# A bidirectional RWKV-7 chunk scan on one Trainium2 core: separate PSUM banks for u and the state increment, an even timetable for two steps, and system transposes on GpSimd

## The chip, the cores and the metric

The kernel runs on one core of a Trainium2 chip. The metric is the device time of one execution in microseconds (us), lower is better. Each kernel is run several times and the median counts; a separate profiled execution supplies the trace from which durations and waits are read.

## The reference

The reference is a two-layer encoder trunk in fp32, applied to a prompt of 256 tokens and a sample of 1024 tokens with the same weights (width 1024, 16 heads of 64). Layer 0 mixes tokens with bidirectional RWKV-7, layer 1 with neighbourhood attention, and each is followed by a squared-ReLU MLP. Only the recurrence of layer 0 matters here; it runs once forwards and once backwards and the two outputs are added:

```
def _wkv_scan(r, w, k, v, a, b, reverse):
    def step(S, inp):
        r_t, w_t, k_t, v_t, a_t, b_t = inp
        sa = jnp.einsum('bhvk,bhk->bhv', S, a_t)
        S = S * w_t[:, :, None, :] + sa[..., None] * b_t[:, :, None, :] + v_t[..., None] * k_t[:, :, None, :]
        return S, jnp.einsum('bhvk,bhk->bhv', S, r_t)
    ...
    _, y = lax.scan(step, s0, seq, reverse=reverse)
...
for d in range(2):
    ...
    y = y + _wkv_scan(rf, _heads(decay), k_d, vf, -kk, kk * iclr, reverse=(d == 1))
...
y = ((y - mu) * lax.rsqrt(var + GN_EPS)).reshape(B, T, C) * lnx_g + lnx_b
y = y + (bonus * vf).reshape(B, T, C)
```

## The kernel before

The program does the trunk stage by stage: projections of RWKV-7, the scan, output projection and MLP, then attention and its MLP. Large products are three fp32r products (`ps<-ah,whi`, `ps<-al,whi`, `ps<-ah,wlo`), lines 95 to 97. The change touches only the scan stage.

The scan turns the recurrence over tokens into one over chunks of 64 tokens. Two heads share 128 partitions. It has ten jobs of 16 steps each: jobs 0 and 1 are the prompt (four head pairs of four chunks each), jobs 2 to 9 the sample (one head pair, 16 chunks each). In a step both directions advance by a chunk, direction d=1 about half a step behind d=0. One step of one direction is this chain:

- `s0` (L989, TensorE): `w` in PSUM receives the masked key products `zk` times the values.
- `sd` (L993, GpSimd): the state `S` times the chunk's decay.
- `s1` (L1000, TensorE): `w` += `ar`·`S`. Then two ACT (ScalarE) copies of `w` into `up` (L1004, in the profile `u<-w`).
- `s2` (L1009, TensorE): `us` = `Q`·`up`, where `Q` is the inverse of the chunk's triangular system. ACT copies it to `hv` (L1011) and, in two pieces by `s2c`, to `u2` (L1018, `u<-us`).
- `s3` (L1023, TensorE): the state increment from `lt` and `hv`. Two DVE (VectorE) operations add it to `sd` and make the new `S` (L1031; L1029 where a sequence begins). The next `s1` needs it.
- `s4` (L1037, TensorE): `w` += `zb`·`u2`. The output rows go to `y`, by ACT (L1040) in the first eight steps of a job, by DVE (L1042) in the last eight.

`us` and the state increment of direction d lie in one PSUM bank, `pbank[d]`, as columns 0 to 127 and 192 to 319.

Between these steps stands work for steps and jobs to come. A group is four chunks of a direction, and every two steps one group of each of these kinds is done: products `aps` (L807) and the DVE mask that makes `zb` (L809); products `kps` (L932), an ACT copy to `zk` (L935) and its GpSimd mask (L937); four transposes `lps` (L945) and the ACT copy `lt` (L948); two merges of small products, `yps` (L893, ACT copies L898) and `qps` (L908, ACT copies L912 into `Q`). The triangular systems of the next job are inverted once per job in 31 rank-1 updates on DVE (`tmp` L847, `q` L849, sizes up to 128x256). Ahead of them four copies transpose the system from `mraw` to `mt` (L836), behind them four more transpose the result to `qt` (L861); `qt` goes to DRAM and twelve DMAs (`qld`) bring it back as `Q` and `qx`. After a job its output is normalised half by half (`scan_post`): DVE and GpSimd work, a reciprocal root that goes between DVE and ACT (L1144, L1156 to L1159), four transposes `zps` (L1131) and an ACT copy `zt` (L1133).

The order is written by hand. Each piece of work is put in a list with a time in steps (`at(t, f)`, job j begins at 16j), the list is sorted, and under `manual_schedule` the instructions of TensorE, DVE, ACT and GpSimd stand in each queue exactly in that order. The numbers are thus no times on the chip; they only set the order, and an instruction at the head of its queue that waits holds all behind it. The DMA queue of SyncE (SP) takes its transfers in that order, too. PSUM tiles `aps`, `kps`, `lps`, `yps`, `qps`, `zps` share two pools of three buffers under one tag.

Of the kernel before, what the change touches and what calls it, by code (L numbers as in the profile page):

```python
# [48 lines left out]
class Trunk:  # L49
# [653 lines left out]
    def scan_begin(self):  # L703
# [11 lines left out]
                                           (("bb", 4), ("ar", 10), ("zb", 10)))  # L715
# [19 lines left out]
    def scan(self):  # L735
# [12 lines left out]
        grow(self.r_bk, fx, "bdk", [P, 4, P], 3)  # L748
# [4 lines left out]
        self.pbank = [self.pw.tile([P, 320], F32, name=f"us{d}") for d in range(2)]  # L753
# [18 lines left out]
    def scan_job(self, j):  # L772
# [13 lines left out]
        for n, (d, g) in enumerate(order):  # L786
# [26 lines left out]
            at(t - (1.614 if j else 7.0), load, E)  # L813
            for c in range(5):
                at(t + (c * 0.133 + -0.013 if c < 4 else 0.577), lambda c=c, f=prod: f(c), E)
            at(t + (1.263 if j else 1.011), store, E)
# [38 lines left out]
        def qst(i):  # L855
            q, r = J["q"], slice(8 * i, 8 * i + 8)
            if i == 0:
                J["qt"] = self.er.tile([P, 32, 32], F32, name="qt", tag="mraw")
                J["qd"] = self.dsc.tile([2, P, 32, 32], F32, name="qd", tag="qd", bufs=2)
                nc.sync.dma_start(J["qd"][0], q)  # L860
            nc.scalar.copy(J["qt"].rearrange("p s t -> p t s")[:, r], q[:, r])  # L861
            if i == 3:
                nc.sync.dma_start(J["qd"][1], J["qt"])
# [20 lines left out]
        for n, (d, g) in enumerate(order):  # L884
            m, c0 = grp[g]

            def merge1(d=d, g=g):
                lo, hi = d, 1 - d
                yps = self.pt.tile([64, 4, 32], F32, name="yps", tag="aps")
                for c in range(4):  # L890
                    for e in range(2):
                        r0 = 64 * e + 32 * lo
                        nc.tensor.matmul(yps[32 * e:32 * e + 32, c, :], J["zb"][d, g][r0:r0 + 32, c, 32 * hi:32 * hi + 32],  # L893
                                         J["qx"][r0:r0 + 32, 4 * g + c, :], start=True, stop=True)
                yt = self.rp.tile([P, 4, 32], F32, name="yt", tag="yt", bufs=2)
                for e in range(2):
                    rh = 64 * e + 32 * hi
                    nc.scalar.copy(yt[rh:rh + 32], yps[32 * e:32 * e + 32])  # L898
                J["yt", d, g] = yt

            def merge2(d=d, g=g):
                lo, hi = d, 1 - d
                Q, yt = J["Q"], J["yt", d, g]
                qps = self.pt.tile([P, 4, 32], F32, name="qps", tag="aps")
                for c in range(4):
                    for e in range(2):
                        rl, rh = 64 * e + 32 * lo, 64 * e + 32 * hi
                        nc.tensor.matmul(qps[rl:rl + 32, c, :], yt[rh:rh + 32, c, :],  # L908
                                         Q[rh:rh + 32, 4 * g + c, d, 32 * hi:32 * hi + 32], start=True, stop=True)
                for e in range(2):  # L910
                    rl = 64 * e + 32 * lo
                    nc.scalar.copy(Q[rl:rl + 32, 4 * g:4 * g + 4, d, 32 * hi:32 * hi + 32], qps[rl:rl + 32])  # L912
            t = 2 * n - 3.992
            at(t + 0.5833, merge1)
            at(t + 2.59, merge2)


            def kload(d=d, g=g, m=m, c0=c0):
                bk = self.rp.tile([P, 4, P], F32, name="bk", tag="bk", bufs=3)
# [7 lines left out]
            def kprod(c, d=d, g=g, n=n):  # L927
# [4 lines left out]
                nc.tensor.matmul(ps[:, c, :], bd[:, c, :], J["ar"][d, g][:, c, :], start=True, stop=True)  # L932
                if c == 3:
                    zk = self.rp.tile([P, 4, P], F32, name="zk", tag="zk", bufs=3)
# [5 lines left out]
            def ktr(c, d=d, g=g, n=n):  # L940
# [4 lines left out]
                nc.tensor.transpose(ps[:, c, :], bk[:, c, :], self.ident)  # L945
                if c == 3:
                    lt = self.rp.tile([P, 4, P], F32, name="lt", tag="lt", bufs=3)
# [25 lines left out]
        for d in range(2):  # L973
            for i in range(16):
# [4 lines left out]
                self.scan_step(at, i + 0.481 * d, J, st[d], d, cc, m, c0 + cc % 4, new, end, i >= 8)  # L979
        self.scan_post(at, J, grp, j == len(self.jobs) - 1)  # L980

    def scan_step(self, at, t, J, st, d, cc, m, ch, new, end, second):
# [23 lines left out]
        def s2():  # L1006

            us = self.pbank[d][:, 0:P]
# [6 lines left out]
        def s2c():  # L1015
            for e in range(2):
                es = slice(64 * e, 64 * e + 64)
                nc.scalar.copy(R["u2"][es, es], self.pbank[d][o:o + 64, es])  # L1018

        def s3():  # L1020

            sn = self.pbank[d][:, 192:320]
# [20 lines left out]
        at(t - 0.22, s0)  # L1043
        if not new and not end:
            at(t - 0.25, sd)
        at(t, s1)
        at(t + 0.33, s2)
        at(t + 0.33 + 0.01, s2c)
        if not end:
            at(t + 0.66, s3)  # L1050
        at(t + 0.82, s4)

    def scan_post(self, at, J, grp, last):

        nc = self.nc
        for half in range(2):
# [71 lines left out]
            def tr(st=st, yb=yb, runs=runs):  # L1128
                ps = self.pt.tile([P, 4, P], F32, name="zps", tag="aps")
                for b in range(4):  # L1130
                    nc.tensor.transpose(ps[:, b, :], yb()[:, b // 2, b % 2, :], self.ident)  # L1131
                zt = self.yp.tile([P, 4, P], F32, name="zt", tag="zt", bufs=1)
                nc.scalar.copy(zt, ps)  # L1133
                for m, k, tb in runs:
                    nc.sync.dma_start(self.scr["z_d"][m, :, tb * P:(tb + 2) * P], zt[:, k:k + 2].rearrange("p b t -> p (b t)"))
            for dt, f in ((-4.0 if tail else -1.5, ld), (-0.186, p1), (0.474, p2), (-0.5 if tail else 1.327, p3a), (1.601, p2b), (-0.4 if tail else 1.982, p3b), (1.843, p2c), (2.252, p3),
                          (3.521, p4), (4.15, p4b), (4.563, p5), (5.809, tr)):
# [787 lines left out]
```

## Time and profile before

| | before |
|---|---|
| median of 3 runs | 4403.65 us (4403.26 to 4409.92) |
| profiled execution, its own time | 4414.36 us |
| its span (first to last instruction) | 4412.6 us |
| mean granted TensorE clock | 0.948 |
| scan stage, first to last `s2` product | 820.2 to 1649.7 us |
| busy, share of the span | PE 92%, DVE 61%, ACT 41%, POOL 38% |

PE is TensorE's products and PEld its weight loads, DVE VectorE, ACT ScalarE, POOL GpSimd, SP the queue that issues most DMAs. A row of a view names the line, the engine, the operation and the tiles (out<-in), how many there were, their busy time and mean duration, and the idle time of the engine just before them with what ended it. A row of the timeline gives start and duration in us, the number of instructions drawn together (x2) and, in brackets, idle time before. A row of the windows gives busy time per engine and the granted clock (PEclk) between two times.

### The profile page before, as it was taken

The page shows a single profiled execution, that of the slowest core. Times are in us where ns is not written, and L with a number is a line of the kernel's source. Part 1 is how long each engine was busy: PE and PEld are TensorE (multiplying, and loading weights), DVE is VectorE, ACT ScalarE, POOL GpSimd, SP SyncE. Part 2 cuts the span into 40 slices and gives each one's busy share as a digit, 9 for nine tenths or more (in the row PEclk, how much of TensorE's full clock was granted, in tenths as well). Part 3 has the DMA queues.
Part 4 walks back from the last instruction along what each step waited for, and adds up shares of the span by engine and source line. Part 5 has one row for each costly group of instructions (what it writes and reads, how often), then busy time and mean ns, then how long its engine had stood idle before and what let it go on. Part 6 is the DMA issues. An engine that isn't in the chain of part 4 may idle for free.

```text
span 4412.6 us, 69989 instructions
## 1 busy us (share of the span) xinstructions
PE 4051.6 (92%) x25060; PEld 3365.7 (76%) x25060; DVE 2684.6 (61%) x5242; ACT 1797.0 (41%) x4785; POOL 1678.7 (38%) x1682
## 2 busy tenths in 40 slices
PE   7888989778888888999999999989998999999999
PEld 4665669667777767788888887977776888888888
DVE  7888873567767745755555556157666565555555
ACT  6764442566777773211111113256555311111111
POOL 5446663234444443422222224044445332222222
PEclk8996779899999999999999999999998999999999
DMA  3234455566566434111111112523334211111111
GB/s 117 81 106 167 167 175 153 149 146 145 139 152 146 116 86 158 58 39 39 39 39 39 39 39 87 167 63 71 77 74 146 86 36 37 39 39 39 39 39 58
DMA packets 484156, 400.27 MB, mean 91 GB/s; under 512 B 289152, under 2 KB 392480, under 8 KB 483808
## 3 DMA queue, kind: packets, MB, share of 16 engines
q1 hardware_dynamic: 447584, 328.56, 27.2%
q10 hardware_dynamic: 34416, 61.35, 3.8%
q0 software_dynamic: 1808, 5.90, 0.4%
q8 instruction: 197, 3.23, 0.3%
q14 instruction: 151, 1.24, 0.1%
HBM read 285.66 MB, written 121.24 MB: 92 GB/s over the span
## 4 chain that ended last, share of the span: by engine, by line
PE 62%; DVE 8%; ACT 6%; DMA 3%; issue 2%; SPq 2%; POOL 2%; ACTq 0%; DVEq 0%; POOLq 0%
PE ps L95 16%; PE ps L96 16%; PE ps L97 16%; PE us L1023 2%; DVE tmp L847 1%; DVE q L849 1%; PE kps L932 1%; PE vps L499 1%; PE op L1840 1%; DVE S L1031 1%; PE us L1009 1%; PE vps L501 1%; PE vps L500 1%; PE pt L1782 1%; PE aps L807 1%
## 5 line engine op out<-in xcount | busy, mean ns | idle before, releaser
L1397 DVE TENSOR_TENSOR x<-ps,x 128x256 f32<-128x256 f32 x1488 | 814.3, 596 | 638.4 <-PE ps L97 638.3
L95 PE MATMUL ps<-ah,whi 128*128 128x512 f32 (+1 forms) x2304 | 848.4, 368 | 4.2 <-ACT whi L89 3.5
L96 PE MATMUL ps<-al,whi 128*128 128x512 f32 (+1 forms) x2304 | 830.3, 360 | 2.6 <-POOL al L1287 2.6
L97 PE MATMUL ps<-ah,wlo 128*128 128x512 f32 (+1 forms) x2304 | 828.3, 360 | 2.1 <-POOL wlo L90 2.0
L90 POOL TENSOR_TENSOR wlo<-raw,whi 128x1024 fp32r<-128x1024 f32 (+1 forms) x178 | 390.4, 2193 | 861.6 <-ACT whi L89 834.2
L95 PE MATMUL ps<-hh,whi 128*128 128x512 f32 (+1 forms) x1536 | 548.3, 357 | 12.0 <-DVE x L1397 11.9
L96 PE MATMUL ps<-hl,whi 128*128 128x512 f32 (+1 forms) x1536 | 547.3, 356 | 0.0
L97 PE MATMUL ps<-hh,wlo 128*128 128x512 f32 (+1 forms) x1536 | 546.4, 356 | 0.0
L95 PEld LDWEIGHTS ps<-ah,whi 128*128 128x128 f32 x2304 | 439.1, 191 | 84.6 <-issue 13.4
L97 PEld LDWEIGHTS ps<-ah,wlo 128*128 128x128 f32 x2304 | 438.3, 190 | 72.3 <-POOL wlo L90 3.0
L96 PEld LDWEIGHTS ps<-al,whi 128*128 128x128 f32 x2304 | 439.3, 191 | 67.2 <-POOL al L1287 2.9
L89 ACT CAST whi<-raw 128x1024 fp32r<-128x1024 f32 (+1 forms) x206 | 200.4, 973 | 708.7 <-PE ps L96 639.0
L1376 POOL TENSOR_TENSOR rl<-rl 128x512 f32<-128x512 f32 (+1 forms) x192 | 174.3, 908 | 504.6 <-PE ps L97 462.5
L95 PEld LDWEIGHTS ps<-hh,whi 128*128 128x128 f32 x1536 | 291.5, 190 | 57.5 <-DVE x L1397 15.1
L1375 ACT ACTIVATE rl<-ps 128x512 f32<-128x512 f32 (+1 forms) x192 | 100.7, 525 | 550.1 <-PE ps L97 550.1
L97 PEld LDWEIGHTS ps<-hh,wlo 128*128 128x128 f32 x1536 | 292.0, 190 | 41.7
L96 PEld LDWEIGHTS ps<-hl,whi 128*128 128x128 f32 x1536 | 291.6, 190 | 40.5
L1378 ACT CAST hh<-rl 128x512 fp32r<-128x512 f32 (+1 forms) x192 | 105.6, 550 | 321.1 <-POOL rl L1376 321.0
L993 POOL TENSOR_TENSOR sd<-S,dall 128x128 f32<-128x128 f32 x256 | 118.4, 462 | 303.1 <-DVE S L1031 244.7
L1031 DVE SCALAR_TENSOR_TENSOR S<-us,dall,sd 64x64 f32<-64x64 f32 x512 | 144.6, 282 | 142.8 <-PE us L1023 75.0
L1379 DVE TENSOR_TENSOR hl<-rl,hh 128x512 fp32r<-128x512 f32 (+1 forms) x192 | 119.3, 621 | 150.4 <-ACT hh L1378 149.9
L1775 POOL TENSOR_TENSOR s<-s,mx 128x384 f32<-128x384 f32 (+1 forms) x154 | 116.9, 769 | 212.1 <-DVE mx L1774 136.5
(310 smaller groups left out, 8750.3 us busy)
## 6 DMA issues: line engine op xcount, KB each, us to landing
raw<-in_w_down_dram SPq DMA_DIRECT2D x64, 512.0 KB, 3.5
raw<-in_w_up_dram SPq DMA_DIRECT2D x64, 512.0 KB, 3.5
ar<-ar_d SPq DMA_DIRECT2D x80, 256.0 KB, 3.4
bk<-bk_d SPq DMA_DIRECT2D x80, 256.0 KB, 3.2
ar_d<-ar ACTq DMA_DIRECT2D x32, 512.0 KB, 2.7
bk_d<-bk ACTq DMA_DIRECT2D x32, 512.0 KB, 3.5
bs<-tab SPq DMA_DIRECT2D x128, 96.0 KB, 3.7
v_d<-vt ACTq DMA_DIRECT2D x80, 128.0 KB, 4.2
```

What stands on the lines that cost most here:

```text
L89: nc.scalar.copy(hi[:, cs], raw)
L90: lo_eng.tensor_tensor(out=lo[:, cs], in0=raw, in1=hi[:, cs].bitcast(F32), op=ALU.subtract)
L95: mm(ps, sh, mh, start=first, stop=False)
L96: mm(ps, sh, ml, start=False, stop=False)
L97: mm(ps, sl, mh, start=False, stop=last)
L993: nc.gpsimd.tensor_tensor(out=R["sd"], in0=st["S"], in1=self.dall[:, m, d, ch:ch + 1].to_broadcast([P, P]), op=ALU.mult)
L1031: nc.vector.scalar_tensor_tensor(out=S2[es, es], in0=sn[es, es], scalar=D, in1=R["sd"][es, es], op0=ALU.mult, op1=ALU.add)
L1376: nc.gpsimd.tensor_tensor(out=r[:, :n], in0=r[:, :n], in1=r[:, :n], op=ALU.mult)
L1378: nc.scalar.copy(hh[:, :n], r[:, :n])
L1379: nc.vector.tensor_tensor(out=hl[:, :n], in0=r[:, :n], in1=hh[:, :n].bitcast(F32), op=ALU.subtract)
L1397: nc.vector.tensor_tensor(out=xv, in0=ps[:, :n], in1=xv, op=ALU.add)
L1775: nc.gpsimd.tensor_tensor(out=s[:, :nk], in0=s[:, :nk], in1=mx[:, 2:3].to_broadcast([P, nk]), op=ALU.mult)
```

## The change

It is made of four parts.

1. `pbank[0]` and `pbank[1]` become `ubank` (all `us`) and `nbank` (all state increments), each shared by both directions.
2. The times change. Of a step: `s0` -0.22 to -0.12, `sd` -0.25 to -0.04, `s2c` 0.34 to 0.51, `s4` 0.82 to 0.717, the lag of d=1 0.481 to 0.5. The four products of a group stand at 0.05, 0.1, 0.27 and 0.43 of a step, `aps` in even steps, `kps` in odd ones; the mask that makes `zb` at 0.45, formerly 0.577 (the rank-1 updates stand at 0.43 of a step before, 0.47 after). The four transposes `lps` stand close together at 0.55 to 0.62. The ACT copies of `zk`, `lt`, `yt`, into `Q`, and `zt` get times of their own, behind the products that they read. `zps` and its copy move to steps 19.72 and 23.72, and the loads of the post-processing from `t0 - 1.5` to `t0 - 0.2`.
3. Buffers: `bb` 4 to 3, `bk` 3 to 2, `bdk` 3 to 2, `zk` and `lt` 3 to 4.
4. The eight transposing copies per job (`mtr` and `qst`, 64x256 and 128x256 fp32, read in rows and written with a stride of 32 elements) go from ACT to GpSimd.

Behind the change the lines of a step are: `s0` L1002, `sd` L1006, `s1` L1013, `up` L1017, `s2` L1022, `hv` L1024, `u2` L1031, `s3` L1036, `S` L1044 (or L1042), `s4` L1050, `y` L1053 and L1055; `kps` L943, `zk` L946 and L948, `lps` L957, `lt` L960, `yt` L902, `Q` L919, `zps` L1144.

```diff
-                                           (("bb", 4), ("ar", 10), ("zb", 10)))
+                                           (("bb", 3), ("ar", 10), ("zb", 10)))
...
-        self.pbank = [self.pw.tile([P, 320], F32, name=f"us{d}") for d in range(2)]
+        self.ubank, self.nbank = (self.pw.tile([P, P], F32, name=nm) for nm in ("us", "sn"))
...
-            at(t - (1.614 if j else 7.0), load, E)
-            for c in range(5):
-                at(t + (c * 0.133 + -0.013 if c < 4 else 0.577), lambda c=c, f=prod: f(c), E)
-            at(t + (1.263 if j else 1.011), store, E)
+            at(t - (1.614 if j else 5.0), load, E)
+            for c, dt in enumerate((0.05, 0.1, 0.27, 0.43, 0.45)):
+                at(t + dt, lambda c=c, f=prod: f(c), E)
+            at(t + 1.0, store, E)
...
-            nc.scalar.copy(J["mt"][64:128].rearrange("p s t -> p t s")[:, r], J["raw"][64:128, r])
+            nc.gpsimd.tensor_copy(J["mt"][64:128].rearrange("p s t -> p t s")[:, r], J["raw"][64:128, r])
...
-        T2 = T1 + (1.8 if j else 2.359)
+        T2 = T1 + (1.84 if j else 2.359)
...
-            nc.scalar.copy(J["qt"].rearrange("p s t -> p t s")[:, r], q[:, r])
+            nc.gpsimd.tensor_copy(J["qt"].rearrange("p s t -> p t s")[:, r], q[:, r])
...
-            t = 2 * n - 3.992
-            at(t + 0.5833, merge1)
-            at(t + 2.59, merge2)
+            t = 2 * n - 4
+            at(t + 0.55, merge1)
+            at(t + 1.2, merge1c)
+            at(t + 2.555, merge2)
+            at(t + 2.7, merge2c)
...
-            at(t - 2.665, kload)
-            for c in range(4):
-                at(t + c * 0.1667 + 0.7067, lambda c=c, f=kprod: f(c))
-                at(t + c * 0.242 + 1.448, lambda c=c, f=ktr: f(c))
+            t = 2 * n - 5
+            at(t - 1.75, kload)
+            for c, (dt, dl) in enumerate(((0.05, 0.55), (0.1, 0.57), (0.27, 0.6), (0.43, 0.62), (0.7, 1.2))):
+                at(t + dt, lambda c=c, f=kprod: f(c))
+                at(t + dl, lambda c=c, f=ktr: f(c))
...
-                self.scan_step(at, i + 0.481 * d, J, st[d], d, cc, m, c0 + cc % 4, new, end, i >= 8)
+                self.scan_step(at, i + 0.5 * d, J, st[d], d, cc, m, c0 + cc % 4, new, end, i >= 8)
...
-            us = self.pbank[d][:, 0:P]
+            us = self.ubank
...
-                nc.scalar.copy(R["u2"][es, es], self.pbank[d][o:o + 64, es])
+                nc.scalar.copy(R["u2"][es, es], self.ubank[o:o + 64, es])
...
-            sn = self.pbank[d][:, 192:320]
+            sn = self.nbank
...
-        at(t - 0.22, s0)
+        at(t - 0.12, s0)
         if not new and not end:
-            at(t - 0.25, sd)
+            at(t - 0.04, sd)
         at(t, s1)
-        at(t + 0.33, s2)
-        at(t + 0.33 + 0.01, s2c)
+        at(t + 0.333, s2)
+        at(t + 0.51, s2c)
         if not end:
-            at(t + 0.66, s3)
-        at(t + 0.82, s4)
+            at(t + 0.667, s3)
+        at(t + 0.717, s4)
```

The first place is TensorE in an odd step of job 2 or later. The names are those above; a number behind a name is the buffer, x2 two instructions in a row. Before:

```order
L1000 MATMUL w_9932<-S1_7181,ar19_7148 128x128
L1023 MATMUL us0_7171<-hv0_6157,lt_9693 128x128
L945 MATMUL lps_9948<-cst_60,bk_9646 128x128
L989 MATMUL w_9961<-v20_6158,zk_9628 128x128
L1009 MATMUL us1_7172<-u10_7177,qq0_6159 128x128
L1037 MATMUL w_9905<-u22_7175,zb18_7157 128x128
L945 MATMUL lps_9948<-cst_60,bk_9646 128x128
L807 MATMUL aps_9973<-ar16_7145,bb0_6160 128x128
L1000 MATMUL w_9961<-S2_7182,ar18_7147 128x128
L807 MATMUL aps_9973<-ar16_7145,bb0_6160 128x128
L1023 MATMUL us1_7172<-hv0_6157,lt_9851 128x128
```

And after:

```order
L1013 MATMUL w_10782<-S3_7180,ar5_6168 128x128
L957 MATMUL lps_10798<-cst_60,bk_10640 128x128 x4
L1036 MATMUL sn_7169<-hv1_7134,lt_10416 128x128
L1050 MATMUL w_10740<-u22_7172,zb4_6177 128x128
L1022 MATMUL us_7168<-u10_7174,qq1_7136 128x128
L1002 MATMUL w_10814<-v21_7135,zk_10393 128x128
L1013 MATMUL w_10814<-S0_7177,ar4_6167 128x128
L807 MATMUL aps_10830<-ar2_6165,bb0_6160 128x128 x2
L1036 MATMUL sn_7169<-hv1_7134,lt_10557 128x128
L1050 MATMUL w_10782<-u23_7173,zb5_6178 128x128
```

In the first rows `s3` (L1023, `us0`) and `s4` of the same direction (L1037, `w_9905`) have a transpose, an `s0` and the other direction's `s2` between them. Now `s4` (L1050) stands right behind its direction's `s3` (L1036) and ahead of the other direction's `s2` (L1022), and the background products stand between `s1` and `s3` (L1013 to L1036).

The second place is ACT, in the last eight steps of a job. Before:

```order
L1011 COPY hv1_7136<-us1_7172 64x128
L1018 COPY u21_7174<-us1_7172 64x64 x2
L1004 COPY u12_7179<-w_11594 64x64 x2
L935 COPY zk_11612<-kps_11590 128x512
L1011 COPY hv1_7136<-us0_7171 64x128
L1018 COPY u22_7175<-us0_7171 64x64 x2
L1004 COPY u10_7177<-w_11618 64x64 x2
```

And after:

```order
L1024 COPY hv1_7134<-us_7168 64x128
L1017 COPY u10_7174<-w_11750 64x64 x2
L1031 COPY u21_7171<-us_7168 64x64 x2
L902 COPY yt_11722<-yps_11713 32x128 x2
L1024 COPY hv1_7134<-us_7168 64x128
L1017 COPY u11_7175<-w_11778 64x64 x2
L1031 COPY u22_7172<-us_7168 64x64 x2
```

The copies into `u2` (L1018, now L1031) stood right behind `hv` of their own step; now the copies into `up` of the other direction (L1017) stand between.

The third place is DVE in a step of rank-1 updates. Before:

```order
L1031 SCALAR_TENSOR_TENSOR S3_7183<-us1_7172,dall_64,sd_11894 64x64 x2
L847 TENSOR_TENSOR tmp_11981<-mt_11663,q_11669 128x231
L849 TENSOR_TENSOR q_11669<-q_11669,tmp_11981 128x21x11
L847 TENSOR_TENSOR tmp_11984<-mt_11663,q_11669 128x240
L849 TENSOR_TENSOR q_11669<-q_11669,tmp_11984 128x20x12
L809 TENSOR_TENSOR zb10_7149<-aps_11945,cst_60 128x512
L1031 SCALAR_TENSOR_TENSOR S0_7180<-us0_7171,dall_64,sd_11927 64x64 x2
```

And after:

```order
L1044 SCALAR_TENSOR_TENSOR S3_7180<-sn_7169,dall_64,sd_11916 64x64 x2
L809 TENSOR_TENSOR zb10_7147<-aps_11961,cst_60 128x512
L847 TENSOR_TENSOR tmp_11983<-mt_11676,q_11682 128x231
L849 TENSOR_TENSOR q_11682<-q_11682,tmp_11983 128x21x11
L847 TENSOR_TENSOR tmp_11986<-mt_11676,q_11682 128x240
L849 TENSOR_TENSOR q_11682<-q_11682,tmp_11986 128x20x12
L1044 SCALAR_TENSOR_TENSOR S0_7177<-sn_7169,dall_64,sd_11947 64x64 x2
```

The mask that makes `zb` (L809) now stands ahead of the rank-1 updates instead of behind them, so DVE comes to the updates only when the fourth product `aps` is there.

More of the change, by code (lines that the diff above doesn't have):

```diff
@@ L747, in scan @@
         self.r_bk, self.r_u2, self.r_u1, self.r_s = [[], 0], [[], 0], [[], 0], [[], 0]
-        grow(self.r_bk, fx, "bdk", [P, 4, P], 3)
+        grow(self.r_bk, fx, "bdk", [P, 4, P], 2)
         self.sp = pool("sp", 4)
@@ L931, in kprod @@
                 ps = J["pk"]
-                nc.tensor.matmul(ps[:, c, :], bd[:, c, :], J["ar"][d, g][:, c, :], start=True, stop=True)
-                if c == 3:
-                    zk = self.rp.tile([P, 4, P], F32, name="zk", tag="zk", bufs=3)
+                if c < 4:
+                    nc.tensor.matmul(ps[:, c, :], bd[:, c, :], J["ar"][d, g][:, c, :], start=True, stop=True)
+                else:
+                    zk = self.rp.tile([P, 4, P], F32, name="zk", tag="zk", bufs=4)
                     nc.scalar.copy(zk, ps)
```

33 lines of the change are left out of this document (21 added, 12 removed).

## The prediction, made before the changed kernel had been run

> **What bounds the kernel now.** I read the page first, for the span, then the rows of one line for the extent of the scan, then the windows for its jobs, the groups for the waits, and the timeline for the chain within a step.
>
> ```profile
> span 4412.6 us, 69989 instructions
> ```
>
> ```profile
> L1009 PE MATMUL us<-u,qq x640: 274/275/581, 820.2 to 1649.7; 128*128 128x128 f32 x160
> ```
>
> The first `s2` starts at 820.2 us and the last at 1649.7. Only these 829.5 us can change much; ten jobs of 16 steps make 83 us a job and 5.2 us a step. The windows hold jobs 2 to 7 (six jobs), then job 5's steps with rank-1 updates (0 to 9) and those without (10 to 15):
>
> ```profile
> 991.50:1495.70 504.20, 418.01 (x4405) 371.69 (x4404) 370.51 (x985) 361.78 (x1441) 229.56 (x361) 0.99 0.62 145
> 1245.80:1301.90 56.10, 46.40 (x469) 40.55 (x467) 47.09 (x119) 38.91 (x156) 25.24 (x38) 0.97 0.53 129
> 1301.90:1330.50 28.60, 23.66 (x273) 21.96 (x272) 14.93 (x47) 21.34 (x86) 12.99 (x23) 1.00 0.80 179
> ```
>
> A middle job is 504.2 / 6 = 84.0 us. With updates a step takes 5.61 us and DVE (the third sum) is busy 84%; without, it takes 4.77 us. No engine is full: a step is a loop of waits between TensorE, ACT and DVE. One of them is what part 1 of the change goes for:
>
> ```profile
> L1023 PEld LDWEIGHTS us<-hv,lt 128*128 128x128 f32 x576 | 88.5, 194 | 68.5 <-ACT u L1018 65.0
> ```
>
> `s3` needs only `hv`, but shares its bank with `us`, and so waits for the copies to `u2`, 65.0 us in all. One such wait, in the order ACT, ACT, TensorE:
>
> ```profile
> 1306.78 0.42 ACT L1018 COPY u<-us 64x64 f32<-64x64 f32 x2
> 1307.22 0.43 ACT L1004 COPY u<-w 64x64 f32<-64x64 f32 x2
> 1307.25 0.30 PEld L1023 LDWEIGHTS us<-hv,lt 128*128 128x128 f32 x2 [0.53 <-ACT u L1018]
> ```
>
> A pair of copies holds ACT for 0.44 us (1306.78 to 1307.22), and TensorE goes on 0.05 us after its end. The prices of the other links are the distances between these rows:
>
> ```profile
> 1252.88 0.30 PEld L1000 LDWEIGHTS w<-S,ar 128*128 128x128 f32 x2 [1.71 <-DVE S L1029]
> ...
> 1253.46 0.43 ACT L1004 COPY u<-w 64x64 f32<-64x64 f32 x2 [1.33 <-PE w L1000]
> ...
> 1254.40 0.36 DVE L847 TENSOR_TENSOR tmp<-mt,q 128x192 f32<-128x192 f32 x1
> 1254.47 0.26 ACT L1011 COPY hv<-us 64x128 f32<-64x128 f32 x1 [0.58 <-PE us L1009]
> ...
> 1255.18 0.58 DVE L1031 SCALAR_TENSOR_TENSOR S<-us,dall,sd 64x64 f32<-64x64 f32 x2
> ...
> 1255.82 0.30 PEld L1000 LDWEIGHTS w<-S,ar 128*128 128x128 f32 x2 [1.01 <-DVE S L1031]
> ```
>
> ```profile
> 1303.36 0.30 PEld L1023 LDWEIGHTS us<-hv,lt 128*128 128x128 f32 x2
> 1303.36 0.49 PE L1023 MATMUL us<-hv,lt 128*128 128x128 f32 x2
> 1303.57 0.30 PEld L932 LDWEIGHTS kps<-ar,bdk 128*128 128x128 f32 x2
> ...
> 1303.95 0.58 DVE L1031 SCALAR_TENSOR_TENSOR S<-us,dall,sd 64x64 f32<-64x64 f32 x2 [0.64 <-PE us L1023]
> 1303.99 0.52 ACT L912 COPY qq<-qps 32x128 f32<-32x128 f32 x2
> ```
>
> So: `s1` to the start of its `up` copies 0.58; `s3` to the `S` update 0.59; `S` update 0.58 and 0.06 to the next `s1`; a product follows the one ahead after about 0.22; copies into `Q` 0.52.
>
> **Part 1 and 2, the banks and the order of a step.** `s3` loses its wait. But `s4` needs `u2`, and two edits work against it: it now stands directly behind `s3`, and on ACT the other direction's `up` now stands ahead of `u2`. Behind the waiting `s4` in TensorE's queue stand the other direction's `s2`, the next `s0`, and the next `s1`. I walked a step with the prices above, from `s1` of d=0 at 0: `up` 0.58 to 1.01, `u2` of d=1 until 1.46, `s4` of d=1 at 1.51; then, 0.22 apart, a product, `s2`, `s0`, a product and `s1` of d=1 at 2.62. The second half is the same with two background products fewer: `up` from 3.20, `u2` of d=0 until 4.08, `s4` at 4.12, `s2`, `s0`, and the next `s1` at 4.78. The loop is 2 x 1.5 + 8 x 0.22 = 4.77 us, and `S` (ready about 3.3 + 0.59 + 0.58 = 4.5) isn't what ends it. TensorE waits about 0.85 and 0.63 us a step at `s4`, where it now waits for the same copies at `s3`: the 65 us don't go, they move, and grow. In even steps the copies into `Q` (0.52) stand behind `u2` and ahead of the next `up`, and `s2` of d=1 needs them: it starts at 4.66 instead of 4.34, so the step is 5.09. Eight of each are 78.9 us a job. The shared banks cost nothing beyond this: `s2` of the other direction overwrites `us` only behind that `s4`, and two state increments stand half a step, 2.4 us, apart, against 1.17 for product and update.
>
> What doesn't fit in the loop, per job:
>
> ```profile
> L809 DVE TENSOR_TENSOR zb<-aps,cst 128x512 f32<-128x512 f32 x63 | 43.6, 692 | 5.6 <-PE aps L807 4.0
> ```
>
> In even update steps `zb` (0.69) now comes first, waits for the fourth `aps`, from 2.96 to 3.57 by the same walk, and then the two updates, then `S`. Two updates are four operations of 0.36 for 192 elements, about 1.5 us, from 0.9 to 1.75 over the sizes. The next `s1` is at 3.57 + r + 0.64; with r = 0.88 that is just 5.09, and only three of the five such steps, taken at r = 1.1, 1.75 and 1.2, are late: +1.4 us. The `zps` transposes, now at places of their own on TensorE's path, are one pass instead of two: eight at 0.11 are +0.9. The clock (0.97 to 1.00 in the windows): +1.0.
>
> The rest of ACT's and DVE's dealings remains. The root of the post-processing ties them together:
>
> ```profile
> L1156 ACT ACTIVATE rqt<-rqx 128x8 f32<-128x8 f32 x19 | 4.0, 209 | 22.1 <-DVE rqx L1144 21.9
> ```
>
> ACT waits 22.1 us for DVE in it, 2.2 a job; since ACT is in the loop twice a step now, half of it is taken as lost: +1.1 (bounds 0 and 2.2). DVE in turn is stretched by GpSimd, in the same operation of the same size:
>
> ```profile
> 1249.96 1.32 POOL L1126 TENSOR_TENSOR y<-y,vt 128x512 f32<-128x512 f32 x1
> ...
> 1250.19 1.27 DVE L847 TENSOR_TENSOR tmp<-mt,q 128x156 f32<-128x156 f32 x1
> ```
>
> ```profile
> 1290.46 0.32 DVE L847 TENSOR_TENSOR tmp<-mt,q 128x156 f32<-128x156 f32 x1
> ```
>
> An update that meets a long GpSimd operation loses 0.95 us. I take three such losses a job as not covered: +2.8 (bounds 0, and six or 5.7). Sum: 78.9 + 1.4 + 0.9 + 1.0 + 1.1 + 2.8 = 86.1 us a middle job against 84.0, six times +2.1.
>
> **Part 3, buffers and loads.** `Q` goes to DRAM and back, and the loads of later groups stand behind these DMAs on SP's queue:
>
> ```profile
> 1301.39 0.32 SPq L863 DMA_DIRECT2D qd<-qt  x1
> ```
>
> ```profile
> 1318.66 0.30 PEld L807 LDWEIGHTS aps<-ar,bb 128*128 128x128 f32 x2 [1.52 <-DMA ar<-ar_d]
> ```
>
> From the store of `qt` to the first `aps` behind that backlog are 17.3 us. The order leaves about that, 3.5 steps or 17.5 us, so I count nothing with what covers it just enough; the row's 1.52 us a job if it doesn't. Fewer buffers of `bb`, `bk` and `bdk` only let the loads start later by a group, two steps or 10 us behind.
>
> **Part 4, the copies on GpSimd.** ACT is relieved of eight copies:
>
> ```profile
> L861 ACT COPY qt<-q 128x256 f32<-128x256 f32 x36 | 21.2, 639 | 9.1 <-DVE q L849 8.6
> ```
>
> They take 0.64 us each there, beside steps 10 and following where ACT is busy 21.3 of 28.6 us; on the loop the walk has them worth nothing, since it has no place for them. GpSimd has room (13.0 of 28.6 us), but no such copy is in this trace. Its only copies are small ones that read with a stride:
>
> ```profile
> L660 POOL COPY dall<-ec 128x8 f32<-128x8 f32 x32 | 20.9, 652 | 0.0
> ...
> L660 POOL COPY dall<-ec 128x4 f32<-128x4 f32 x16 | 6.1, 381 | 0.0
> ```
>
> They give (652 - 381) / 4 = 68 ns an element. The other end is ACT's 0.64 us. I take 0.65, since the new copies read whole rows and only write with a stride; two masks of `zk` and an `sd` stand between the last of the four, so `qt` comes later than from ACT by the length of these; that delay is inside B's price. The Trainium skill's "GPSIMD Engine Reference", section 7 "Performance pitfalls for Q7 kernels", says that many small read commands cost about 102 cycles each without overlap, which agrees with the 68 ns an element for strided reads and would spare copies that read in rows; no run so far shows one of those.
>
> **Sum.** Six middle jobs +12.6 us; jobs 0 and 1 together +1, since they have less in their steps; job 8, which prepares no `zb`, 0; job 9, which has the walk's loop without the updates but now the post-processing in its even slots, +2. That is +15 us, put on the profiled execution's 4414.4 us (10.7 above the median) and on the median alike: 4403.65 + 15 = about 4419.
>
> **Rivals.**
>
> *A, faster: the loop stands at its floor.* If the lost halves above (root, locks, late `zb`, clock) lie in the 0.85 and 0.63 us that TensorE waits at `s4` anyway, a middle job is 78.9 + 0.9 = 79.8, six times -4.2 = -25, and jobs 0, 1 and 8 some -3 each: about -35 us, 4369. For it speaks that the loop then has slack on DVE of over half a microsecond in odd steps, and that before's steps 10 to 15 ran 4.77 us with no update. Against it speaks that before's update steps took 5.61, with DVE busy 84%, and nothing of DVE's work is taken away. It decides if DVE's late operations stay under the slack of the step that they fall in. Chance 0.30.
>
> *B, slower by contention.* The eight copies come out slower, about 1 us, or block DVE where post-processing and updates run. Eight times 0.35 are 2.8 us a job in the chain that ends in `Q`, ten jobs +28, so about 4447. If each of the eight cost DVE its full 0.65, it were 5.2 a job, or 4471. Chance 0.18. The Trainium skill's "SBUF — State Buffer", section "Who interferes with whom", speaks against part 4: DVE operations with two SBUF inputs and GpSimd operations that read SBUF exclude each other for a whole instruction. The trace agrees (1.27 against 0.32 us).
>
> *C, the copies go at 68 ns an element.* Then 256 elements take 17.4 us, eight of them 139 us a job, and with GpSimd's 38.2 us of the quoted job 177 us against 86. Nine jobs wait for their system: some 820 us, 4419 + 820 = about 5240. Chance 0.10.
>
> **How the numbers follow.** The forecast, a loop that gives back at `s4` what it gains at `s3`, has 0.42. Within 0.2% (8.8 us, about what a measurement of this kernel can tell from no change) lies the lower part of its spread (locks and root at their bounds move the sum by some 20 us either way): 0.12. Faster is A, 0.30; slower is the rest of the forecast, B and C, 0.58. The range, 4355 to 4475, holds the forecast, most of A and nearly all of B, and leaves C out.
>
> **What would show it.** Right: TensorE idle at L1050 for ACT's L1031 of over 150 us, none at L1036; odd steps without updates near 4.8 us and even ones near 5.1; POOL copies L861 near 0.65 us; L847 and L849 together no less than before. Wrong: idle at L1050 under 100 us, or update steps as short as the others (A); copies of 1 us and more with L807 waiting for DMA (B); copies of many microseconds (C).

## The result, and the profile after

The changed kernel took 4411.68 us (median of 20 runs, 4405.75 to 4425.36) against 4408.02 us of before in as many runs. The ratio is 1.0013, 95% interval 1.0006 to 1.0020: slower by 0.13%, which is less than the 0.2% that the prediction counts as no change. The profiled executions have spans of 4414.8 and 4412.6 us. All ratios below are to the kernel before on the same chip.

Read in the order of the prediction. First the extent of the scan, by the rows of `s2`:

```profile
L1022 PE MATMUL us<-u,qq x640: 275/275/582, 816.2 to 1651.6; 128*128 128x128 f32 x160
```

The scan begins 4.0 us earlier and ends 1.9 us later. Job by job, from one first `s2` to the next (job 9: to the last `s2`), job 0 takes 81.1 us instead of 85.8, job 1 86.1 instead of 85.5, job 8 81.4 instead of 82.0, and job 9 81.1 instead of 71.9. The windows hold jobs 2 to 7, then steps 0 to 3 of job 5 and its steps 4 to 15:

```profile
983.30:1489.10 505.80, 430.73 (x4405) 372.92 (x4405) 368.28 (x984) 353.80 (x1393) 250.15 (x409) 0.99 0.60 143
1236.40:1260.50 24.10, 19.09 (x189) 16.11 (x188) 22.32 (x55) 15.86 (x64) 11.90 (x18) 1.00 0.44 120
1260.50:1320.20 59.70, 52.49 (x551) 45.79 (x550) 38.99 (x111) 43.14 (x170) 29.79 (x51) 1.00 0.67 158
```

A middle job is 505.8 / 6 = 84.3 us, before 84.0. In steps 0 to 3 DVE (third sum) is busy 22.3 of 24.1 us; the rest of the job runs at 59.7 / 12 = 4.98 us a step. The third last number is the granted clock; over the six jobs it is 0.99 in both kernels.

The groups show where TensorE waits now. In these rows the idle time stands behind the second bar, with what ended it:

```profile
L1050 PEld LDWEIGHTS w<-u,zb 128*128 128x128 f32 x634 | 96.5, 192 | 152.1 <-ACT u L1031 151.4
...
L1013 PEld LDWEIGHTS w<-S,ar 128*128 128x128 f32 x576 | 89.5, 196 | 32.9 <-DVE S L1044 18.8 <-DVE S L1042 12.8
L1036 PEld LDWEIGHTS sn<-hv,lt 128*128 128x128 f32 x574 | 88.7, 195 | 9.4 <-ACT hv L1024 4.6
```

`s3` (L1036) waits 9.4 us where it waited 68.5, and not for `u2`; `s4` (L1050) waits 152.1 us, 151.4 of them for `u2`. Two stretches of the timeline show how, on ACT and on TensorE's weight loads:

```profile
1266.58 0.43 ACT L1017 COPY u<-w 64x64 f32<-64x64 f32 x2 [0.47 <-PE w L1013]
1267.04 0.42 ACT L1031 COPY u<-us 64x64 f32<-64x64 f32 x2
```

```profile
1267.51 0.30 PEld L1050 LDWEIGHTS w<-u,zb 128*128 128x128 f32 x2 [0.55 <-ACT u L1031]
1267.73 0.30 PEld L1022 LDWEIGHTS us<-u,qq 128*128 128x128 f32 x2
1267.95 0.30 PEld L1002 LDWEIGHTS w<-v,zk 128*128 128x128 f32 x2
1268.17 0.30 PEld L1013 LDWEIGHTS w<-S,ar 128*128 128x128 f32 x2
```

One direction's `up` (1266.58) goes ahead of the other's `u2` (1267.04); `s4` starts 0.05 us after `u2`'s end, and `s2`, `s0` and `s1` follow 0.22 us apart, `s1` making the next `up` start. That is the loop that the prediction walked.

Another wait has gone, whose change the prediction put at nothing: that of the products `aps` for the load of `ar`, first before the change and then behind it:

```profile
L807 PEld LDWEIGHTS aps<-ar,bb 128*128 128x128 f32 x498 | 77.7, 200 | 17.5 <-DMA ar<-ar_d 17.1 <-issue 0.3
```

```profile
L807 PEld LDWEIGHTS aps<-ar,bb 128*128 128x128 f32 x496 | 70.3, 192 | 3.0 <-DMA ar<-ar_d 1.8 <-issue 1.2
```

All of it stands in step 13 of a job. In jobs 0 and 1 it was 6.6 and 3.7 us, and their step 13 falls from 12.1 and 9.3 us to 5.6 and 5.1.

### The profile page after: what moved, and what is told of

It reads as the page before. It is cut to its first block, busy times and chain, and to the rows that moved or that the text cites. A ratio compares the mean times of both kernels' runs of the same rounds, so it can differ in the third digit from the quotient of the medians.

```text
span 4414.8 us, 69779 instructions
## 1 busy us (share of the span) xinstructions
PE 4067.2 (92%) x25060; PEld 3365.2 (76%) x25060; DVE 2682.9 (61%) x5242; ACT 1783.1 (40%) x4705; POOL 1714.0 (39%) x1760
## 4 chain that ended last, share of the span: by engine, by line
PE 64%; ACT 7%; DVE 6%; issue 3%; DMA 2%; POOL 2%; SPq 1%; ACTq 0%; DVEq 0%; POOLq 0%
PE ps L95 16%; PE ps L96 16%; PE ps L97 16%; PE w L1050 2%; ACT u L1031 2%; ACT u L1017 2%; PE w L1013 1%; PE us L1022 1%; PE vps L499 1%; PE vps L500 1%; PE vps L501 1%; PE w L1002 1%; PE pt L1799 1%; PE op L1857 1%; DVE tmp L847 1%
## 5 line engine op out<-in xcount | busy, mean ns | idle before, releaser
L1050 PE MATMUL w<-u,zb 128*128 128x128 f32 x640 | 158.9, 331 | 96.7 <-ACT u L1031 95.4
L1044 DVE SCALAR_TENSOR_TENSOR S<-sn,dall,sd 64x64 f32<-64x64 f32 x512 | 145.0, 283 | 147.0 <-PE sn L1036 133.7
L1006 POOL TENSOR_TENSOR sd<-S,dall 128x128 f32<-128x128 f32 x256 | 114.5, 447 | 260.8 <-DVE S L1044 191.1
L1050 PEld LDWEIGHTS w<-u,zb 128*128 128x128 f32 x640 | 97.8, 193 | 154.3 <-ACT u L1031 153.6
```

The source lines that it names most:

```text
L1006: nc.gpsimd.tensor_tensor(out=R["sd"], in0=st["S"], in1=self.dall[:, m, d, ch:ch + 1].to_broadcast([P, P]), op=ALU.mult)
L1044: nc.vector.scalar_tensor_tensor(out=S2[es, es], in0=sn[es, es], scalar=D, in1=R["sd"][es, es], op0=ALU.mult, op1=ALU.add)
L1050: nc.tensor.matmul(w, J["zb"][d, g][:, c, :], R["u2"], start=False, stop=True, skip_group_check=True)
```

## The experiments

**One order at a time.** The first four kernels each change one thing by itself: three in the changed kernel, one (the banks) in the kernel before.

```diff
-        at(t + 0.51, s2c)
+        at(t + 0.34, s2c)
```

> The changed kernel with the copies into u2 at t + 0.34, right behind hv and ahead of the other direction's up copies; TensorE's order is unchanged. Theory of the prediction (a step is the loop up, u2 of the other direction, s4, s1): s4 finds u2 done, the loop becomes s3, S, s1, walked at 3.85 to 4.0 us in odd steps without updates against 4.8, steps 0 to 3 (DVE full) as they are; 12 steps a job lose 0.6 to 0.8 us, 60 to 90 us in all, about 4320 to 4350, and TensorE's idle time at s4 (154 us) falls below 50. Rival (the loop's length comes from the S update or from TensorE's product rate, and the wait at s4 only fills the gap): the wait moves to s1 on DVE's S, steps stay at 4.8 and 5.1, within 10 us of the changed kernel.

Measured: 4357.92 us, ratio 0.9879 (0.9855 to 0.9903), 54 us less than the changed kernel. In the groups:

```profile
L1050 PEld LDWEIGHTS w<-u,zb 128*128 128x128 f32 x636 | 100.2, 199 | 7.3 <-ACT u L1031 6.4
...
L1013 PEld LDWEIGHTS w<-S,ar 128*128 128x128 f32 x574 | 89.4, 196 | 92.0 <-DVE S L1044 72.6 <-DVE S L1042 19.1
```

The wait at `s4` is gone, and part of it is now at `s1`, which waits for `S`. In job 5, steps 5, 9 and 11 take 3.9 us, as walked, and step 7 takes 4.7; the even steps 4 to 10 take 4.3 to 4.9. Steps 0 to 3 together stay at 24.1 us. The gain is a little under the range given, mostly because step 12 of job 5 went from 5.1 to 7.3 us, and on the mean of jobs 2 to 7 from 5.4 to 7.1 (below). This settles the main point: the loop through ACT sets most steps from 4 on, and this one time in the list is worth about 55 us.

```diff
-        at(t + 0.717, s4)
+        at(t + 0.9, s4)
```

> The changed kernel with s4 at t + 0.9 instead of t + 0.717: on TensorE it stands behind the other direction's s2 and the next s0, ACT's order of u2 and up is unchanged. Theory: the same loop is opened on TensorE's side, so s2 no longer stands behind the waiting s4, and odd steps without updates fall to about 3.9 to 4.1; 50 to 90 us less than the changed kernel, about 4320 to 4360. Rival (S update or product rate set the step): no gain, within 10 us, with the wait at s1 on S.

Measured: 4413.97 us, ratio 1.0011 (0.9998 to 1.0023), no gain. In this kernel the normalisation of the first half takes the mean of `y` before one chunk of d=1 has been added. The wait has moved again:

```profile
L1050 PEld LDWEIGHTS w<-u,zb 128*128 128x128 f32 x638 | 99.9, 198 | 0.6 <-ACT u L1031 0.6
L1022 PEld LDWEIGHTS us<-u,qq 128*128 128x128 f32 x636 | 97.5, 193 | 150.2 <-ACT u L1031 112.5 <-ACT qq L919 36.3
```

`s4` waits for nothing, but `s2` of the other direction waits 112.5 us for the same copies: both directions' `us` are the same columns of `ubank`, and `u2` is still being read from them. The theory's sentence that the loop opens on TensorE's side was wrong. The rival's number holds, its mechanism does not: `s1` waits 38.3 us, little more than the 32.9 of the changed kernel. With one `us` for both directions `u2` holds `s2` even when `s4` is out of the way. Of the two orders tried, only ACT's opened the loop; a `us` of its own for each direction, with this late `s4`, wasn't tried.

```diff
-        self.pbank = [self.pw.tile([P, 320], F32, name=f"us{d}") for d in range(2)]
+        self.ubank, self.nbank = (self.pw.tile([P, P], F32, name=nm) for nm in ("us", "sn"))
```

> The kernel before with only the banks changed (u and state increment each in a bank of its own, shared by both directions); times, buffers and engines as before. Theory: there s4 stands one to three products behind s3, so the 68.5 us that s3's weight load waits for u2 mostly go and only part comes back at s4: 20 to 50 us faster than before, about 4360 to 4390. Rival (another wait, s1 on S or s2 on up, takes over in the same step): within 10 us of before.

Measured: 4396.97 us, ratio 0.9975 (0.9963 to 0.9987), about 11 us faster than before. The wait at `s3` falls from 68.5 to 29.1 us, but the gain is nearer to the rival's; `s2` waits more (62.3 us in place of 44.4). The last of these rows is that of before:

```profile
L1023 PEld LDWEIGHTS sn<-hv,lt 128*128 128x128 f32 x574 | 87.3, 192 | 29.1 <-ACT hv L1011 24.2
```

```profile
L1009 PEld LDWEIGHTS us<-u,qq 128*128 128x128 f32 x638 | 97.6, 193 | 62.3 <-ACT u L1004 48.6 <-ACT qq L912 10.4
```

```profile
L1009 PEld LDWEIGHTS us<-u,qq 128*128 128x128 f32 x640 | 100.0, 197 | 44.4 <-ACT u L1004 36.7 <-ACT qq L912 6.7
```

In the two profiled executions jobs 2 to 7 take 502.2 us instead of 504.2, and most of the gain lies in jobs 8 and 9 (75.1 and 69.3 us instead of 82.0 and 71.9); why there is open. The wait for the load of `ar` at L807 is still 19.4 us here.

The last of the four puts the transposing copies back on ACT; shown is the line for `qt`, that for `mt` changes likewise:

```diff
-            nc.gpsimd.tensor_copy(J["qt"].rearrange("p s t -> p t s")[:, r], q[:, r])
+            nc.scalar.copy(J["qt"].rearrange("p s t -> p t s")[:, r], q[:, r])
```

> The changed kernel with the eight transposing copies per job back on ACT; nothing else differs. Theory: on GpSimd they cost 0.63 us each, as on ACT (0.64), beside other work, so part 4 is worth little: within 10 us of the changed kernel, about 4405 to 4422, with ACT's waits shifted in steps 9 to 11 only. Rival (ACT is in the loop twice a step, so each copy in ACT's queue delays the loop by its 0.64 us): 8 x 0.64 = 5 us a job, some +45 us, about 4455.

Measured: 4428.19 us, ratio 1.0047 (1.0035 to 1.0059), some 15 us more than the changed kernel. It lies between the two theories: step 9 takes 6.2 us instead of 4.8 and step 15 5.9 instead of 4.5, that is 1.4 us for each four copies of 0.64 us. About half of ACT's time in them is on the loop. So part 4 did save time, and its copies cost on GpSimd what they cost on ACT. The row is the changed kernel's; on ACT it was 21.2 us and 639 ns:

```profile
L861 POOL COPY qt<-q 128x256 f32<-128x256 f32 x36 | 21.2, 628 | 3.1 <-PE kps L943 2.7 <-DVE q L849 0.4
```

**The extras of the sum.** The next three ask for the terms that the prediction added to its walk.

```diff
-            for c, dt in enumerate((0.05, 0.1, 0.27, 0.43, 0.45)):
+            for c, dt in enumerate((0.05, 0.1, 0.27, 0.43, 0.69)):
```

> The changed kernel with the mask that makes zb at 0.69 of its step, behind the S update of d=0 instead of ahead of the rank-1 updates. Theory of the prediction (in steps 0, 2 and 8 zb and the two updates stand ahead of S and make it late, 1.4 us a job): those steps shorten, 1 to 1.5 us a job, 10 to 15 us in all, about 4397 to 4402. Rival (in steps 0 to 3 DVE's whole queue is full, 22.3 of 24.1 us, and zb delays the next half instead): nothing within 4 us.

Measured: 4423.94 us, ratio 1.0042 (1.0027 to 1.0057), about 13 us slower than the changed kernel. In job 5 steps 0 and 2 fall by 0.3 and 0.4 us, steps 1 and 3 grow by 0.4 and 0.8: there the rival's mechanism fits, DVE's queue is full and `zb` only moves the delay. Its number, nothing within 4 us, does not hold. Steps 12 and 14 grew as well (6.0 and 6.1 us instead of 5.1 and 5.3 in job 5); why is open.

> The changed kernel without four GpSimd operations of the post-processing (mean subtraction, scaling by the root, weight and the addition of the bonus) in jobs 0 to 8, which leaves the output unnormalised; DVE's and ACT's work and all orders stay. Theory (rank-1 updates that meet a long GpSimd operation lose about 0.95 us each, three a job): the updates' operations fall from 250 us in all to about 215, and steps 0 to 3 of a job from 24.1 to about 21.5, some 2.5 us a job, 20 us in all, about 4390. Rival (DVE's own work sets these steps, or a loss is taken up by waits elsewhere): the operations get shorter, but the steps stay within 0.5 us, about 4407 to 4412.

Measured: 4392.56 us, ratio 0.9968 (0.9955 to 0.9981), about 20 us less than the changed kernel. Its window over steps 0 to 3 of job 5, and the updates of the changed kernel and then of this one:

```profile
1224.70:1246.50 21.80, 18.63 (x188) 15.92 (x187) 19.58 (x54) 15.74 (x64) 7.62 (x13) 1.00 0.50 132
```

```profile
L847 DVE TENSOR_TENSOR tmp<-mt,q 128x135 f32<-128x135 f32 (+15 forms) x275 | 127.8, 465 | 6.3
L849 DVE TENSOR_TENSOR q<-q,tmp 128x135 f32<-128x135 f32 (+15 forms) x275 | 122.6, 446 | 9.5
```

```profile
L849 DVE TENSOR_TENSOR q<-q,tmp 128x156 f32<-128x156 f32 (+15 forms) x274 | 117.1, 427 | 9.4
L847 DVE TENSOR_TENSOR tmp<-mt,q 128x175 f32<-128x175 f32 (+15 forms) x273 | 109.3, 400 | 6.3
```

Steps 0 to 3 take 21.8 instead of 24.1 us, and the updates 226.4 instead of 250.4 us in all. DVE's busy time in these steps falls from 22.3 to 19.6 us. So GpSimd's long operations cost 2.3 us a middle job through DVE, the one extra that the runs confirm near its size (2.8). It is what the Trainium skill's "SBUF — State Buffer", section "Who interferes with whom", says of DVE operations with two SBUF inputs: they contend with GpSimd operations that read SBUF.

```diff
+            for i in range(8, 16):
+                for c, dt in enumerate((0.05, 0.1, 0.27, 0.43)):
+                    at(i + dt, lambda c=c: fill(c))
```

Here `fill` is one product of the identity with itself into an unused tile.

> The changed kernel with four products more in each of the last eight steps of job 9, at the slots where the other jobs have their background products; their results are not used. Theory (job 9 took 80.9 us instead of 71.5 because the granted clock fell to 0.50 between about 1627 us and the end of the scan, with few products in TensorE's queue there): the clock stays near 1.00 until the last step, job 9 takes 72 to 75 us, and the whole is 6 to 9 us faster than the changed kernel, about 4403 to 4406. Rival (the last steps are long by the post-processing and the casts of the next stage on ACT and DVE): job 9 stays at 79 to 83 us or grows.

Measured: 4412.78 us, ratio 1.0016 (1.0007 to 1.0025), no gain. The windows from step 12 of job 9 to near the end of the scan, first of the changed kernel, then of this one, then of the kernel with the copies back on ACT, which has no added products (the third last number is the clock):

```profile
1628.00:1652.00 24.00, 19.52 (x88) 16.57 (x88) 11.00 (x31) 12.30 (x46) 10.18 (x14) 0.50 0.09 29
```

```profile
1637.00:1657.00 20.00, 14.00 (x113) 12.02 (x114) 11.06 (x31) 12.72 (x49) 10.43 (x13) 1.00 0.11 34
```

```profile
1643.00:1660.00 17.00, 10.77 (x81) 8.61 (x82) 10.26 (x29) 11.02 (x42) 10.40 (x13) 1.00 0.13 40
```

The clock stays at 1.00 with the products, but that doesn't show that the products keep it there: with the copies on ACT, and in the kernel without the GpSimd operations, TensorE has the changed kernel's order throughout job 9 and no added products, and the clock stays at 1.00 until 2.5 and 4.7 us before the end of the scan, too. There steps 0 to 11 take 58.0 and 57.7 us and the rest of job 9 takes 18.8 and 19.4; in the changed kernel they take 58.0 and 23.1. So the low clock costs job 9 about 4 us. The added products cost something as well: with them steps 0 to 11 take 59.5 us, the rest 18.8, and job 9 78.3 us, not 72 to 75. Why the clock fell in one execution and not in the others is open; in the kernel with the late mask, with the same order in job 9, it fell at 1645 us, also at step 12.

**A version that beats both.** The kernel with `u2` ahead still lost time at step 12, where the weight loads of `kps` (L943) sat idle for 23.9 us over the scan; the profile puts 2.0 of them to the DMA of `bdk` and 21.9 to nothing that it shows. Three edits to the order of loads and two to their queue followed.

> The kernel with u2 ahead of up (s2c at t + 0.34), and the loads of bk and bdk a step earlier (t - 2.75), so that one of them stands ahead of the twelve DMAs that bring Q back instead of behind them. Theory (step 12 of a job took about 7 us instead of 4.4 because kps waits for bdk behind these DMAs on SP's queue): step 12 falls to about 4.5 to 5 us, 2 us a job, 15 to 22 us less than with u2 ahead alone, about 4336 to 4343. Rival (the DMA that ends last there is another, or the next one then waits): step 12 stays above 6 us, within 6 us of 4358.

Measured: 4371.69 us, ratio 0.9923 (0.9906 to 0.9939). Step 12 falls to 4.4 us, which shows that it waited for these loads. The rival's second half (the next one then waits) holds for the rest: step 13 rises from 5.0 to 8.8 us on the mean of jobs 2 to 7 (11.0 in job 5), waiting for `ar` and `bb`, and the time is 14 us above 4358, more than the rival said.

> The kernel with u2 ahead of up, and three edits to the order on SP's queue: bk and bdk a step earlier (t - 2.75), ar and bb a step earlier (t - 2.6), and the loads of the first half's post-processing ahead of the twelve DMAs of Q (t0 - 3.2) instead of behind them. Theory (after the earlier kload alone, step 13 took 9 to 11 us since ar and bb stood behind all the rest; SP's queue is busy without a gap from the store of qt for some 20 us, so what counts is what stands behind the twelve DMAs): steps 12 and 13 take 4.5 to 5.5 us each, a middle job 75 to 77 us instead of 80, 20 to 35 us less than with u2 ahead alone (4358), about 4325 to 4340. Rival (the queue as a whole is too slow, and the next load in line waits whatever the order): steps 12 to 14 sum as before, within 10 us of 4358.

Measured: 4357.07 us, ratio 0.9893 (0.9879 to 0.9908), the rival's time again. Steps 12 and 13 are mostly short now (4.4 and 5.5 us on the mean of jobs 2 to 7), but the system's loads come later, and DVE's first update waits for the copy of them (17.0 us over the scan, 6.8 with `u2` ahead alone):

```profile
L847 DVE TENSOR_TENSOR tmp<-mt,q 128x175 f32<-128x175 f32 (+15 forms) x273 | 125.4, 459 | 17.0 <-POOL mt L836 9.1 <-DMA ar<-ar_d 1.8
```

Step 0 of job 5 takes 9.2 us where it took 5.8. In these two kernels whatever stands last on SP's queue is late.

> The same as the kernel with the reordered loads, but the post-processing's second half five steps later (its GpSimd operations in steps 6 to 11 of the next job instead of 1 to 6), and the first half's GpSimd operations up to a step earlier. Theory (the long GpSimd operations lengthen the rank-1 updates, and steps 0 to 3 with them, as the kernel without them showed: 21.8 against 24.1 us): steps 0 to 3 fall by 1.5 to 2.3 us, less what DVE's post-processing adds to steps 6 to 9, some 10 to 20 us in all against the kernel with the reordered loads. Rival (in steps 6 to 9 the same operations meet the single large updates and the S updates and cost there what they cost before): within 5 us.

Measured: 4403.22 us, ratio 0.9993 (0.9984 to 1.0003), far worse than its base. The same wait at L847 grows to 35.9 us (step 0 of job 5 takes 12.3), and steps 6 to 8 take 5.9, 5.9 and 8.4 us with the moved work in them, 5.6 us more than with the reordered loads on the mean of jobs 2 to 7. Steps 1 to 3 fall by 3.1 us. Both the theory and the rival thus have something for them, but the longer wait in step 0 may itself shorten the steps behind it, so this run doesn't separate the two.

The last two take six of the twelve DMAs from SP:

```diff
+            eng = (nc.sync, nc.gpsimd)[ds[0]]
...
         at(T3 + 1.1, qld)
+        at(T3 + 1.8, lambda: qld((1,)))
```

> The kernel with u2 ahead of up, and six of the twelve DMAs that bring Q and qx back issued from ACT's queue at 0.7 steps later, the other six from SP's as before. Theory (SP's queue, which issues one DMA after the other at about 0.5 us each, is what steps 12 and 13 wait for): SP's backlog is 3.3 us shorter, step 12 falls from about 7 to 4.5 to 5.5, ACT pays about 6 x 0.4 = 2.4 us a job in steps 11 and 12 of which part is in the loop; 5 to 20 us less than 4358, about 4338 to 4353. Rival (the transfers themselves, not their issue, are the limit): step 12 stays near 7 and ACT's six issues come on top, 4358 to 4375.

Measured: 4359.94 us, ratio 0.9893 (0.9878 to 0.9908). Step 12 is short (4.2 us in job 5), and `kps` no longer waits, but step 11 takes 8.6 us instead of 3.9: on ACT the six issues stand in the loop. So step 12 does what the theory said, and the time is still the rival's.

> The same with the six DMAs issued from GpSimd's queue. Theory (SP's issue is the limit): step 12 falls to 4.5 to 5.5; what GpSimd pays for an issue isn't in the traces so far, with about 1 us each it delays sd in steps 11 and 12 by some us; about 4335 to 4358. Rival (the transfers are the limit): step 12 near 7, 4358 or more.

Measured: 4342.64 us, ratio 0.9855 (0.9838 to 0.9871), the best of all: 65 us less than before and 69 less than the changed kernel. The timeline has the six issues on GpSimd:

```profile
1254.40 2.59 POOL L878 DMA_DIRECT2D qq<-qd  x4 [1.28 <-DMA qd<-qt]
```

```profile
1256.99 1.29 POOL L883 DMA_DIRECT2D qx<-qd  x2
```

They take 0.65 us each and GpSimd waits 1.28 us ahead of them. The wait at `kps` falls from 23.9 to 3.8 us. Step 12 falls to 5.5 us in job 5 (7.3 with `u2` ahead alone), on the mean of jobs 2 to 7 only from 7.1 to 6.3, and step 13 from 5.0 to 4.0. SP's queue is thus what step 12 waited for, at least in part: the transfers are the same, and moving six of them to either other queue ends the wait. Whether what counts is the time that SP takes to issue them, or how the transfers of one queue follow each other, isn't separated.

## Why the prediction was right

It forecast 4419, in a range from 4355 to 4475, slower by 15 us as the likeliest case; measured is slower by 3.7, a quarter of it. That is within the 0.2% that the prediction itself counts as no change, to which it gave a chance of 0.12. The mechanism, a loop that gives back at `s4` what it gains at `s3`, holds. That the total came out so near is partly luck, since errors in both directions cancel: in the profiled executions the scan ends 1.9 us later, made of -4.0 for its start, -4.2 for jobs 0 and 1, +1.6 for jobs 2 to 7, -0.6 for job 8 and +9.2 for job 9, where the sum had 0, +1, +12.6, 0 and +2. Point by point:

- **The loop at `s4`: right, in kind and in numbers.** Over 150 us of wait at L1050 were forecast, 152.1 measured; none at L1036, 9.4 measured; 4.8 and 5.1 us for odd and even steps, and the steps of job 5 from 4 on are 5.0, 4.8, 5.1, 5.2, 5.3, 4.8, 4.9, 4.8 and so on. The kernel with `u2` ahead shows that it is this loop and its price.
- **The extras of a middle job: too large.** The sum said 86.1 us, the windows 84.3. For steps 0 to 3 the walk gave 19.7 and the extras that belong there (1.1 of late `zb`, half of the 1.1 of the root, since one of a job's two roots stands in step 3 and the other in step 14, and 2.8 of locks) made 24.2; measured 24.1. There the total is right, though not all its parts: locks 2.3 by experiment; the `zb` term is no price of its own, since moving it gained nothing in a full queue. For steps 4 to 15 the walk gave 59.2, and 59.7 were measured: most of the extras there, 0.9 for `zps` and 1.0 for the clock among them, had no place. Six jobs thus gave +1.6 us, not +12.6. One sign of being right failed, too: L847 and L849 together were to take no less than before, and take 250.4 us instead of 258.1.
- **Jobs 0 and 1, and the start: wrong by 9 us.** A loss of 1 us was forecast; the scan began 4.0 us earlier and jobs 0 and 1 took 4.2 less. Two steps failed, "jobs 0 and 1 together +1" and, under Part 3, "I count nothing" for the loads behind `Q`. The wait for `ar` in step 13 was 6.6 and 3.7 us in these jobs, not the 1.5 of the quoted row; behind the change it is 1.3 and none, and 6.6 and 4.1 us less in step 13 outweigh what the other steps gained in length. In the kernel with the banks alone, whose times are those of before, it is still 6.8 and 3.5 us, so it is not the banks. In job 0 SP issues the load of `ar` 12.8 us behind the store of `qt`, before 17.8; which of the moved times or buffers did this wasn't tried by itself. The start varies: 813.3 to 817.0 us in the profiled executions of the seven kernels with the changed times and no edit to the loads, 820.2 and 817.2 with those of before. The prediction had no term for it.
- **Job 9: mis-sized.** +2 forecast, +9.2 measured. Up to step 11 the job takes 58.0 us instead of 55.7, which is the +2. The rest takes 23.1 instead of 16.2: about 4 us by the clock, which fell to 0.50 at 1628 us and in the kernel before only in its last step, and the other 3 by the order of the last steps. In the two executions whose clock stayed at 1.00 with the same order, job 9 took 76.8 and 77.1 us, so part of the +9.2 belongs to this one execution.
- **Part 4: the price of a copy right (0.63 against 0.65 us), its worth wrong.** "Worth nothing on the loop" failed; it is worth 15 us, since ACT is in the loop. Rival C is ruled out: what copies that read with a stride cost per element didn't carry over to copies that write with one. The prediction's link from these 68 ns to the cost of small read commands was an inference that no run shows.
- **Part 3**, the buffers, wasn't tried by itself.
- **Rival A** is half true: the walk's floor was met from step 4 on, but steps 0 to 3 are DVE's. **Rival B** is not: the copies run at 0.63 us.

The parts that were tried by themselves are some -11 us for the banks, -15 for the copies on GpSimd, and +54 for `u2` behind `up`. They sum to +28, not to the 3.7 measured. So some -24 us belong to the parts that weren't tried alone (the other times, the loads, the buffers; the wait for `ar` alone fell by 15 us), or the parts don't add up; the runs don't tell how much is which.

## What to carry to other kernels

Where two chains share an in-order engine, the place of each small copy in its queue can be worth more than the resource conflict that one removes: after taking a wait away, walk the next round of the loop and see which instruction the waiting one now holds. When a wait moves with every reordering (from `s3` to `s4` to `s2`), look for the shared thing behind it, here ACT's order and one `us` in PSUM. And a queue that issues without a gap has to be shortened; reordering it only chose who was late here.

## What the runs showed of the hardware that was not expected

- The granted clock fell to 0.50 at step 12 of the scan's last job in two executions (at 1628 us in the changed kernel; TensorE was busy 7.69 of the 10 us from 1615 on) and stayed at 1.00 until 2.5 and 4.7 us before the scan's end in two others whose TensorE has the same order in this job. The order of instructions alone doesn't decide it.
- A GpSimd copy of 128x256 fp32 that reads rows and writes with a stride of 32 elements took 0.63 us, though copies of 8 and 4 elements that read with a stride had taken 0.65 and 0.38.
- A DMA issued from GpSimd's queue held it for 0.65 us, about as long as one held SP's (four of its six in 2.54 us in the same execution).
